# Loading the last y in two halves, and going over all PSUM banks once per half, in a batched matmul with transposed x

One Trainium2 chip, one core of it, one launch. The metric is the device time in microseconds of that core; the kernel before takes 261.97 us (median of 6 runs, 261.90 to 262.24).

## What is computed

```python
batch, m, k, n = 16, 512, 768, 1024
x: (batch, k, m) float32      y: (batch, k, n) float32
return np.einsum('bkm,bkn->bmn', x, y).astype(np.float32)
```

Inputs and output are float32 in HBM; the products are taken in bf16, which the comparison allows.

## The kernel before

PE is the matrix engine, DVE the vector engine, ACT the scalar engine; SP issues the transfers, which sixteen DMA engines carry out. PSUM is the memory, in banks, into which PE writes its sums. A transfer has *landed* when the last of the sixteen engines has reported its part. The *granted clock* is PE's clock as a share of full speed.

For each of 16 batches: x (1.57 MB) and y (3.15 MB) are loaded as one transfer each, cast to bf16 by DVE (one instruction for x, two for the halves of y), multiplied by PE into eight PSUM banks (six steps of the contraction for each), copied from PSUM by ACT, and stored (2.10 MB). All transfers are issued in program order by the SP queue. Stores are *held back*: that of batch b-4 is issued after the loads of batch b (`LAG`), so the loads never queue behind a store that is not ready yet.

```python
LAG = 4
...
for b in range(B):
    xs = xs_pool.tile([P, KT, M], FP32, name="xs")      # 2 buffers
    ys = ys_pool.tile([P, KT, N], FP32, name="ys")      # 2 buffers
    nc.sync.dma_start(xs[:], x_v[b])
    nc.sync.dma_start(ys[:], y_v[b])
    if b >= LAG:
        store(b - LAG)
    ...
    nc.vector.tensor_copy(x_sb[:], xs[:])
    for h in range(2):
        ks = slice(h * KT // 2, (h + 1) * KT // 2)
        nc.vector.tensor_copy(y_sb[:, ks], ys[:, ks])
    ...
    for mo in range(MT):                                # 4
        for nt in range(NT):                            # 2
            ns = slice(nt * NF, (nt + 1) * NF)
            ps = psum.tile([P, NF], FP32, name="ps")    # 8 banks
            for kt in range(KT):                        # 6
                nc.tensor.matmul(ps[:], x_w[:, kt, mo], y_sb[:, kt, ns],
                                 start=(kt == 0), stop=(kt == KT - 1))
            nc.scalar.copy(o_sb[:, mo, ns], ps[:])
for b in sorted(o_tiles):                               # the last LAG stores
    store(b)
```

## Time and profile before

| | kernel before |
|---|---|
| device time, median | 261.97 us |
| span of the profiled execution | 260.1 us |
| PE / DVE / ACT busy | 74% / 32% / 29% |
| share of the sixteen DMA engines | 98.5% |
| traffic | 109.05 MB |
| last y has landed | 235.0 us |
| last store issued, landed | 251.3 us, 259.2 us |

Three things to know when reading it. The span runs to the end of the program's last instruction, so the final wait for the stores is in it; the device time is about 1.9 us longer. The chain of waits ends earlier, with the last instruction that counts as busy, the last PSUM copy at 251.3. Waiting for a store and moving its data do not count: what the queue does after that copy has to be read from the windows and from the times that transfers take to land. And a transfer's issue is short (0.33 us) while its landing is late: the time in between contains everything that stood before it in the queue.

### The profile page before, as it was taken

What the parts mean: (1) busy time and instruction counts of PE and PEld (TensorE: products, weight loads), DVE (VectorE), ACT (ScalarE), POOL (GpSimd) and SP (SyncE); (2) the same over time, 40 slices, a digit from 0 to 9 for tenths busy, and PEclk for the clock granted to TensorE, in tenths of its full rate; (3) what the DMA queues carried; (4) which work ended last, traced back from release to release, by engine and by line L of the source; (5) the groups of instructions that cost most, each with busy time, mean ns of one, the idle gap of its engine ahead of it and who ended that gap; (6) DMA issues with size and microseconds to landing.
All of it is one profiled execution on the core that took longest, in us unless ns stands there. A gap on an engine that the chain in (4) does not pass through costs nothing.

```text
span 260.1 us, 1877 instructions
## 1 busy us (share of the span) xinstructions
PE 192.3 (74%) x768; PEld 89.3 (34%) x768; DVE 83.0 (32%) x48; ACT 76.4 (29%) x129; POOL 0.2 (0%) x4
## 2 busy tenths in 40 slices
PE   0059999896947939599597886939779395895950
PEld 0014555353523514235143342514334142351420
DVE  0271643525213252222524215252132522225000
ACT  1003444342421403314123241413324042141330
POOL 0000000000000000000000000000000000000000
PEclk9999999999997998959779797997999899796895
DMA  7999999999999999999999999999999999999995
GB/s 299 427 423 420 438 433 427 431 369 422 430 430 432 432 430 435 430 432 423 433 435 421 438 422 438 429 427 437 435 424 424 432 431 430 437 425 432 431 408 242
DMA packets 6921, 109.18 MB, mean 420 GB/s; under 512 B 768, under 2 KB 768, under 8 KB 768
## 3 DMA queue, kind: packets, MB, share of 16 engines
q1 hardware_dynamic: 6912, 109.05, 98.5%
q8 instruction: 6, 0.10, 0.1%
q14 instruction: 3, 0.02, 0.0%
HBM read 75.50 MB, written 33.55 MB: 419 GB/s over the span
## 4 chain that ended last, share of the span: by engine, by line
DMA 80%; DVE 10%; PE 5%; DVEq 1%; SPq 0%; issue 0%; ACT 0%
DMA ys<-in_y_dram 80%; DVE y_sb L65 10%; PE ps L74 5%; DVEq L106 1%; SPq L56 0%; ACT o_sb L76 0%; SPq L57 0%; DVEq L65 0%
## 5 line engine op out<-in xcount | busy, mean ns | idle before, releaser
L74 PE MATMUL ps<-y_sb,x_sb 128*128 128x512 bf16 x768 | 192.3, 413 | 58.4 <-DVE y_sb L65 58.4
L74 PEld LDWEIGHTS <-x_sb 128*128 128x128 bf16 x768 | 89.3, 118 | 160.9 <-issue 47.5
L76 ACT COPY o_sb<-ps 128x512 f32<-128x512 f32 x128 | 75.2, 587 | 174.1 <-PE ps L74 174.1
L65 DVE CAST y_sb<-ys 128x3072 bf16<-128x3072 f32 x32 | 54.9, 1757 | 89.4 <-DMA ys<-in_y_dram 89.4
L62 DVE CAST x_sb<-xs 128x3072 bf16<-128x3072 f32 x16 | 28.2, 1760 | 66.2 <-DMA xs<-in_x_dram 55.2
L76 ACT ACT_TABLE_LOAD x1 | 1.3, 1283 | 0.7 <-PEq L95 0.7
L95 POOL MEMSET const-uint8-127<- 128x1 uint8 x1 | 0.1, 103 | 0.0
L95 POOL MEMSET const-bfloat16-1.0<- 128x1 bf16 x1 | 0.1, 102 | 0.0
L95 POOL MEMSET const-float32-1.0<- 128x1 f32 x1 | 0.1, 100 | 0.0
L95 POOL MEMSET const-float32-0.0<- 128x1 f32 x1 | 0.1, 99 | 0.2 <-issue 0.2
## 6 DMA issues: line engine op xcount, KB each, us to landing
ys<-in_y_dram SPq DMA_DIRECT2D x16, 3072.0 KB, 28.1
out_dram<-o_sb SPq DMA_DIRECT2D x16, 2048.0 KB, 32.6
xs<-in_x_dram SPq DMA_DIRECT2D x16, 1536.0 KB, 29.7
```

The lines of the kernel that those rows point to most:

```text
L62: nc.vector.tensor_copy(x_sb[:], xs[:])
L65: nc.vector.tensor_copy(y_sb[:, ks], ys[:, ks])
L74: nc.tensor.matmul(ps[:], x_w[:, kt, mo], y_sb[:, kt, ns], start=(kt == 0), stop=(kt == KT - 1))
L76: nc.scalar.copy(o_sb[:, mo, ns], ps[:])
L95: nc = _bacc.Bacc("TRN2", target_bir_lowering=False, num_devices=1)
L106: with _tile.TileContext(nc) as tc:
```

## The change

The intent: at the end of the program nothing is left to load, so the last batch's cast, matmuls and copies stand alone (16.3 us after the last y). If its y comes in two halves, PE can do the first half of the contraction for all eight banks while the second half is still arriving.

```diff
+    KH = KT // 2
...
-            nc.sync.dma_start(xs[:], x_v[b])
-            nc.sync.dma_start(ys[:], y_v[b])
+            halves = 2 if b == B - 1 else 1
+            load(xs[:], x_v[b], 1)
+            for h in range(halves):
+                ks = slice(h * KT // halves, (h + 1) * KT // halves)
+                load(ys[:, ks], y_v[b, :, ks], 1)
...
-            for mo in range(MT):
-                for nt in range(NT):
-                    ns = slice(nt * NF, (nt + 1) * NF)
-                    ps = psum.tile([P, NF], FP32, name="ps")
-                    for kt in range(KT):
-                        nc.tensor.matmul(ps[:], x_w[:, kt, mo], y_sb[:, kt, ns],
-                                         start=(kt == 0), stop=(kt == KT - 1))
-                    nc.scalar.copy(o_sb[:, mo, ns], ps[:])
+            ps = {}
+            for h in range(halves):
+                for mo in range(MT):
+                    for nt in range(NT):
+                        if h == 0:
+                            ps[mo, nt] = psum.tile([P, NF], FP32, name="ps")
+                        for kt in range(h * KT // halves, (h + 1) * KT // halves):
+                            mm(ps[mo, nt], x_w, y_sb, kt, mo, nt)
+                        if h == halves - 1:
+                            nc.scalar.copy(o_sb[:, mo, nt * NF:(nt + 1) * NF], ps[mo, nt][:])
```

`load` and `mm` are the old calls under a name. Batches 0 to 14 are built as before.

More of the change, by code (lines that the diff above doesn't have):

```diff
@@ L45, with load, mm @@
     LAG = 4
+    KH = KT // 2
     o_tiles = {}
+    def load(dst, src, rows):
+        nc.sync.dma_start(dst, src)
     def store(b):
         nc.sync.dma_start(o_v[b], o_tiles.pop(b)[:])
+    def mm(ps, x_w, y_sb, kt, mo, nt):
+        nc.tensor.matmul(ps[:], x_w[:, kt, mo], y_sb[:, kt, nt * NF:(nt + 1) * NF],
+                         start=(kt == 0), stop=(kt == KT - 1))
     with tc.manual_schedule():
@@ L63 @@
             for h in range(2):
-                ks = slice(h * KT // 2, (h + 1) * KT // 2)
+                ks = slice(h * KH, (h + 1) * KH)
                 nc.vector.tensor_copy(y_sb[:, ks], ys[:, ks])
@@ L68 @@
             o_tiles[b] = o_sb
-            for mo in range(MT):
-                for nt in range(NT):
-                    ns = slice(nt * NF, (nt + 1) * NF)
-                    ps = psum.tile([P, NF], FP32, name="ps")
-                    for kt in range(KT):
-                        nc.tensor.matmul(ps[:], x_w[:, kt, mo], y_sb[:, kt, ns],
-                                         start=(kt == 0), stop=(kt == KT - 1))
-                    nc.scalar.copy(o_sb[:, mo, ns], ps[:])
-            if False:
-                store(b)
+            ps = {}
[8 more added lines that the diff above has]
+                            nc.scalar.copy(o_sb[:, mo, nt * NF:(nt + 1) * NF], ps[mo, nt][:])
         for b in sorted(o_tiles):
```

## The prediction

> **What bounds the kernel now.** I read the page from the top: engines, the DMA row, the chain of waits. Then I left the averages and went to the last 30 us, the only stretch that the change touches.
>
> ```profile
> span 260.1 us, 1877 instructions
> PE 192.3 (74%) x768; PEld 89.3 (34%) x768; DVE 83.0 (32%) x48; ACT 76.4 (29%) x129; POOL 0.2 (0%) x4
> DMA  7999999999999999999999999999999999999995
> q1 hardware_dynamic: 6912, 109.05, 98.5%
> HBM read 75.50 MB, written 33.55 MB: 419 GB/s over the span
> ```
>
> No compute engine is above 74%, while the sixteen DMA engines are busy in every slice between the first and the last, 98.5% of the span. 109.05 MB at the 430 GB/s of the middle slices is 253.6 us of a 260.1 us span. So the kernel is bound by its traffic, and the change moves the same bytes. A gain can come only from the 6.5 us that are not full-rate traffic: the start, and the end.
>
> The chain of waits, in order of time, cut to its end, seems to promise such a gain:
>
> ```profile
> 206.94 28.08 DMA ys<-in_y_dram
> 235.03 0.03 issue
> ...
> 235.12 1.76 DVE y_sb L65
> 236.88 1.68 DVEq L106
> 238.56 0.04 issue
> 238.60 12.09 PE ps L74 x45
> 250.69 0.02 issue
> 250.71 0.59 ACT o_sb L76
> ```
>
> The last y lands at 235.03, and 16.3 us of cast, matmuls and PSUM copies follow before the last store can be issued. But this chain ends with the last counted instruction, at 251.3; the span ends at 260.1, and the chain does not say what the queue carried between 235 and 260. Two further views do: the windows of the tail, and the stores that were issued in it.
>
> ```profile
> 219.30:235.03 15.73, 12.30 (x48) 5.63 (x48) 5.18 (x3) 4.70 (x8) 0.00 (x0) 0.89 1.01 432
> 235.03:251.00 15.97, 13.54 (x48) 5.76 (x48) 3.43 (x2) 4.40 (x8) 0.00 (x0) 0.79 1.00 426
> 251.00:252.50 1.50, 0.00 (x0) 0.00 (x0) 0.00 (x0) 0.29 (x1) 0.00 (x0) 1.00 0.85 360
> 252.50:257.00 4.50, 0.00 (x0) 0.00 (x0) 0.00 (x0) 0.00 (x0) 0.00 (x0) 0.59 0.97 411
> 257.00:258.60 1.60, 0.00 (x0) 0.00 (x0) 0.00 (x0) 0.00 (x0) 0.00 (x0) 0.50 0.29 123
> ```
>
> ```profile
> L50 SPq DMA_DIRECT2D out_dram<-o_sb x2: 333/333/333, 234.9 to 251.3; - x2
> ...
> DMA to landing us min/median/max: 7.9/13.7/19.5
> ```
>
> ```profile
> SPq L106 <- DMA out_dram<-o_sb: 7.3, 2, 4.8
> ```
>
> In the windows the last two figures are the DMA share and GB/s (before them stand the busy times, with their counts, and the granted clock). While PE works off the last batch, the queue runs at a share of 1.00: stores are held back by four batches, so those of batches 11 to 14 stand behind the last load and are written meanwhile. The second fence is two stores: that of batch 14, issued at 234.9, landing 19.5 us later at 254.4, and that of batch 15, issued at 251.3, landing 7.9 us later at 259.2. The third says the same from the other side: at the end the queue waits twice for stores, the longest 4.8 us, which is 259.2 less 254.4. A store is 2.097 MB, and at 432 GB/s that is 4.85 us. So the last store followed the one before it at the full rate: the queue, not the 16.3 us of compute, sets the end.
>
> **What the Trainium skill says.** "Perfetto Trace Analysis", section DMA Optimizations, makes splitting of transfers conditional: "If DMA engines are generally idle" smaller sections may let the task end sooner. Here they are not: 1.00 in the tail. "DMA: Bandwidth & Descriptors", section Queues, rings and completion order, says that each DMA engine takes its descriptors in ring order and that one copy is split over up to 16 rings. The trace agrees on the order: y of batch 13 landed at 203.39 by the chain, and behind it stood a store, x and y, then again a store, x and y; at 432 GB/s these take 2 x (4.85 + 3.64 + 7.28) = 31.5 us, which gives 234.9 for the last y, measured 235.03. "TensorE: Matmul & The Clock Gate", section What's actually happening, has two clocks, half after idleness and full after activity. The tail agrees in kind: after 2.70 us without matmuls, less than the page's window of some 3.4 us, the granted clock is 0.50 from 237 to 243, which stretches the last batch. "PSUM — Partial Sum Buffer", section The four PSUM rules, says the first matmul of a group clears the write bits of its whole bank. Eight groups open at once are therefore safe only with a bank each; 512 fp32 columns are one 2 KB bank and the pool has eight. No run shows it yet.
>
> **The change part by part.** Batches 0 to 14 keep instructions, transfers and order. I compared the built order of instructions: PE 768 matmuls and as many weight loads in both, ACT 128 copies, DVE 48 casts; only the DMA queue gets one more transfer, 49 in place of 48.
>
> 1. The last y as two transfers of 1.57 MB. These have the shape of an x load: 12 KB a partition and 8 partitions for each DMA engine. In the trace's packet records the median packet of 12 KB takes 460 ns, that of 24 KB 912 ns, so each engine takes 16 x 460 = 7.36 us in place of 8 x 912 = 7.30 us: +0.06 us, on the path. The issue, 0.33 us, lies under a backlog of 28 us.
>
> 2. The first half lands 16 x 460 / 2 = 3.7 us before the second: 231.4. DVE is idle there (its previous cast ended at 229.6), so its 1.76 us cast ends at 233.2. The second half lands at 235.1 and is cast by 236.9.
>
> 3. PE is in batch 14 until 234.2. Now the first 24 matmuls of batch 15 follow at once, not at 236.9. At full clock six matmuls take 1.29 us (copies of the steady part start 1.29 us apart), 0.216 each: 24 x 0.216 = 5.2 us, until 239.4. The second half has been cast for 2.5 us by then, so the other 24 run on to 244.6. Without the gap the clock should stay up; the old last batch took 13.8 us from 236.9, now 10.4 us from 234.2.
>
> 4. Copies: a bank is complete every 3 x 0.216 = 0.65 us and its copy takes 0.587 us, so ACT keeps up, the last ending at about 245.3. The last store is issued 6.0 us earlier than now.
>
> 5. None of these 6.0 us lies on what sets the end. The stores of batches 11 to 14 last until 254.4 whatever PE does, so the last store waits in the ring until its turn, and lands at 259.24 + 0.06 = 259.3. The sum: 261.97 + 0.06 = 262.03 us, in round figures 262.0.
>
> **The rivals.** *The compute tail shows in full.* Then 6.0 us go: 256 us, faster by 2.3%. For it: the chain of waits, whose last 16 us are compute. Against it: the share of 1.00 until 251 and the 4.8 us between the last two landings. With 8 MB of stores behind the last load I give it almost nothing.
>
> *The dip is recovered.* From 251.0 to 252.5 the rate falls to 360 GB/s: the last store came after the quickest engines had run dry. Missing are (431 - 360) x 1.5 us = 0.11 MB, 0.25 us of the whole queue. The change issues the store long before that and closes the dip. If the sixteen engines shared their work it would be worth 0.2 to 0.3 us, 261.7. Against it: each has a fixed share of the partitions, and the slowest decides. In the per-engine landings of the trace the first engine finishes store 14 at 251.4, the last at 254.4; that last one never ran dry, having landed store 13 at 249.56, store 14 at 254.41 and store 15 at 259.24, 4.85 and 4.83 us apart. Closing the dip makes fifteen engines wait longer for the sixteenth.
>
> *PE gets slower.* Every bank is visited twice, and the second visits may wait. If all 48 matmuls ran at half clock (0.43 us) from 234.2, PE would end at 254.8 and the last store be issued at 255.4; with its 7.9 us it would land at 263.3, 4 us late (266, 1.6% slower). Nothing speaks for that clock over 20 busy microseconds; there are 6 us of slack to the first engine's need and nearly 9 to the last one's.
>
> *Another share-out among the DMA engines.* The 3 us between first and last engine grew from 0.6 us at the start, in steps of about a microsecond on single engines. The page has 9 packets of the queues of kind "instruction"; if these cause the steps and fall otherwise in the new program, the slowest engine may end half a microsecond sooner or later.
>
> **Range and chances.** Predicted 262.0 us. Three runs of the kernel before lie within 0.2 us; adding 0.3 downwards for the dip and about 0.3 either way for the share-out gives 261.6 to 262.4. Two per cent would be 5.2 us, more than anything but the fallen first rival can give. Faster by over 2%: 0.01. Within 2%: 0.98. Slower: 0.01.
>
> **What would show it right or wrong.** Right: DVE casts the first half at about 231.4 and PE shows no gap near 235; last PSUM copy ends near 245.3 and the queue issues the last store there, but its time to landing grows from 7.9 to about 14 us; the last two landings stay 4.8 us apart; no dip near 251, with the fall of the rate at the very end starting over a microsecond earlier. Wrong: a span shorter by much more than 0.3 us with the last store landing well before 259, or any stretch of the tail where the queue was empty before the change, which I overlooked.

## The result

| | before | after |
|---|---|---|
| device time, median of 6 | 261.97 us (261.90 to 262.24) | 262.20 us (262.08 to 262.60) |
| ratio after / before | | 1.0008, 95% interval 0.9995 to 1.0021 |
| span of the profiled execution | 260.1 us | 260.5 us |
| last PSUM copy ends | 251.3 us | 245.65 us |
| last store issued | 251.3 us | 245.7 us |
| last store landed | 259.24 us | 259.63 us |

The same, then; the result is correct, with eight sums open at once in a bank each. Ratios are the mean time of one kernel's fast runs over that of the other's of the same rounds, so they are not quite the ratio of the medians quoted.

The chain of waits of the changed kernel, its last part (start, length, what):

```profile
219.63 3.44 DVE y_sb L78 x2
223.07 0.04 issue
223.11 21.93 PE ps L56 x93
245.04 0.02 issue
245.07 0.58 ACT o_sb L93
```

Before, this chain passed through the last load and its casts. Now the loads of the last batch are not in it: PE runs 93 matmuls without a wait from batch 14 into batch 15, and the last copy ends 5.65 us earlier. The timeline of the same stretch (start, length, engine, instruction; in brackets the idle time before it):

```profile
228.19 1.76 DVE L75 CAST x_sb<-xs 128x3072 bf16<-128x3072 f32 x1 [5.13 <-DMA xs<-in_x_dram]
...
231.85 1.76 DVE L78 CAST y_sb<-ys 128x3072 bf16<-128x3072 f32 x1 [1.91 <-DMA ys<-in_y_dram]
...
235.32 10.69 SPq L53 DMA_DIRECT2D out_dram<-o_sb  x2
235.44 1.76 DVE L78 CAST y_sb<-ys 128x3072 bf16<-128x3072 f32 x1 [1.83 <-DMA ys<-in_y_dram]
240.58 5.07 ACT L93 COPY o_sb<-ps 128x512 f32<-128x512 f32 x8 [5.29 <-PE ps L56]
```

Both casts lie under PE's work, and the eight copies follow one another. Everything that was wanted of PE, DVE and ACT happened. Now the queue: the windows that the prediction showed, of the changed kernel (the last two figures are DMA share and GB/s, before them the granted clock), then the two last stores, then the wait at the end:

```profile
235.03:251.00 15.97, 10.00 (x47) 4.99 (x45) 1.76 (x1) 4.96 (x9) 0.00 (x0) 0.89 1.02 433
251.00:252.50 1.50, 0.00 (x0) 0.00 (x0) 0.00 (x0) 0.00 (x0) 0.00 (x0) 0.50 0.92 393
...
257.00:258.60 1.60, 0.00 (x0) 0.00 (x0) 0.00 (x0) 0.00 (x0) 0.00 (x0) 0.50 0.31 133
```

```profile
L53 SPq DMA_DIRECT2D out_dram<-o_sb x2: 332/332/332, 235.3 to 245.7; - x2
...
DMA to landing us min/median/max: 13.9/16.7/19.5
```

```profile
SPq L121 <- DMA out_dram<-o_sb: 13.4, 1, 13.4
```

The last store is issued at 245.7 in place of 251.3 and takes 13.9 us to land in place of 7.9: 245.7 + 13.9 = 259.6. What PE gave, the queue took back as waiting; the queue's issuer now waits 13.4 us in one piece at the end. The engine that lands last had landed the store before at 254.81, 4.82 us earlier, the time of one store at full rate, as before (254.41, then 4.83). (These are the last of the sixteen landings of each store. That they belong to one engine is inferred, since a landing does not name its engine: the last but one keeps its distance, about 0.37 us over the last three stores before the change and about 0.44 us after.) The windows count a packet at its start, so they are uneven over a microsecond or two; the landings are the better evidence.

### The profile page after: what moved, and what is told of

It is laid out like the page before. It is cut to its first block, busy times and chain, and to the rows that moved or that the text cites. A ratio compares the mean times of both kernels' runs of the same rounds, so it can differ in the third digit from the quotient of the medians.

```text
span 260.5 us, 1879 instructions
## 1 busy us (share of the span) xinstructions
PE 191.3 (73%) x768; PEld 89.3 (34%) x768; DVE 83.1 (32%) x48; ACT 76.4 (29%) x129; POOL 0.2 (0%) x4
## 4 chain that ended last, share of the span: by engine, by line
DMA 74%; DVE 11%; PE 8%; issue 0%; ACT 0%; SPq 0%; DVEq 0%
DMA ys<-in_y_dram 74%; DVE y_sb L78 11%; PE ps L56 8%; ACT o_sb L93 0%; SPq L50 0%; DVEq L78 0%
```

## Experiments

If the compute tail is only hidden, and not without effect, it must show as soon as less is queued behind the last load. So the first four runs hold stores back by two batches in place of four. Two stores then stand behind the last y instead of four, and the loads end 9.8 us later (244.80 against 235.03 in the profiles). The rival is that the change gives nothing even there, because its halves do not overlap. The runs also take the change apart.

### 1. Kernel before, hold-back of two

```diff
-    LAG = 4
+    LAG = 2
```

> The kernel before, but stores held back by two batches in place of four, so two stores (batches 13 and 14) in place of four stand behind the last load. My theory (four queued stores hide the compute tail): loads end 2 x 4.85 us later, at 244.7; the old tail of 16.3 us puts the last store's issue at 261.0, and it lands 6.1 us later (the engines that had run dry took 6.1 us in the kernel before), at 267.1; with the 2.7 us between last landing and device time, 269.8 us (269 to 271). Rival (the tail costs nothing in any case): 262.

Measured: 269.33 us (268.47 to 270.83), 1.0289 of the kernel before (1.0247 to 1.0332). The windows of its tail, then its last two stores:

```profile
250.00:255.00 5.00, 5.00 (x25) 2.61 (x23) 0.00 (x0) 2.35 (x4) 0.00 (x0) 1.00 0.48 203
255.00:258.00 3.00, 3.00 (x16) 1.47 (x13) 0.00 (x0) 1.18 (x2) 0.00 (x0) 1.00 0.00 0
```

```profile
L50 SPq DMA_DIRECT2D out_dram<-o_sb x2: 332/338/343, 244.6 to 258.9; - x2
...
DMA to landing us min/median/max: 7.0/8.5/9.9
```

Here is the stretch that the kernel before does not have: from 255 to 258 the DMA moves nothing, 0 GB/s, while PE is busy throughout. The loads ended at 244.80 (expected 244.7), the last store was issued at 258.9 rather than 261.0, because PE's clock was at 1.00 in this execution's tail. Of the four runs two took 268.5 and two 270.2 and 270.8. That they are the ones with the halved clock is not shown: their mean clocks over the whole span, 0.899 and 0.901, are no lower than those of the two faster runs (0.891 and 0.903).

### 2. Changed kernel, hold-back of two

`LAG = 2` here too, in the changed kernel.

> The changed kernel with stores held back by two batches. My theory: the change does shorten the tail by about 5.7 us and here it shows: last store issued at about 255.4, landing 261.5, 264.2 us (263.5 to 265), that is 2% faster than the kernel before at the same hold-back. Rival (the change gives nothing even where the tail is exposed, because the halves do not overlap): 270, as the old one at two.

Measured: 264.44 us (263.29 to 265.34), 1.0094 (1.0056 to 1.0132).

```profile
250.00:255.00 5.00, 5.00 (x25) 2.63 (x24) 0.00 (x0) 3.49 (x6) 0.00 (x0) 1.00 0.48 205
255.00:258.00 3.00, 0.70 (x4) 0.12 (x2) 0.00 (x0) 1.20 (x3) 0.00 (x0) 1.00 0.41 175
```

```profile
L53 SPq DMA_DIRECT2D out_dram<-o_sb x2: 332/338/344, 246.0 to 256.4; - x2
...
DMA to landing us min/median/max: 6.3/7.4/8.6
```

The store resumes in the window where the old order stood still. The change is worth 4.9 us of the medians (269.33 - 264.44; expected 5.6), 1.8%, once the tail is exposed. Both kernels' runs fall into two groups, so compare like with like: fastest with fastest 5.2 us (268.47, 263.29), slowest with slowest 5.5 us (270.83, 265.34). The two profiles shown differ by only 3.2 us (268.47, 265.25), because the old order was caught with the clock up in its tail and the new one with a clock of 0.65 from 235 to 240. The rival falls.

### 3. and 4. Either half of the change alone, hold-back of two

Both edits are to the changed kernel, with `LAG = 2`.

Only the load in halves (PE bank by bank):

```diff
+            halves = 1
             for h in range(halves):
                 for mo in range(MT):
```

> Two batches held back; the last y in two transfers, but PE goes bank by bank as before. One half of the change alone. My theory: only the cast of the first half moves off the path (1.7 us), PE still waits for the second half's cast before its fourth matmul: 268.1 us, or down to 266 if PE's clock stays up over the shorter gap. If splitting the load were all that matters: 264.

Only PE's two passes (one load):

```diff
-            halves = 2 if b == B - 1 else 1
+            halves = 1
...
+            halves = 2 if b == B - 1 else 1
             ps = {}
```

> Two batches held back; the last y in one transfer, PE in two passes over the banks. The other half of the change alone. My theory: PE can only use the 1.7 us of the second half's cast, at half clock, where it did 3 matmuls and now does about 4: 269.5 us, 0.3 us or so below the old order. If the order of the passes were all that matters: 264.

Measured: load alone 267.91 us (266.18 to 268.25), 1.0216; passes alone 269.10 us (268.82 to 269.19), 1.0272. The chains of waits, PE's piece in the last batch, first of the old order (experiment 1), then of the load alone, then of the passes alone:

```profile
248.37 9.89 PE ps L74 x45
```

```profile
246.59 11.57 PE ps L56 x45
```

```profile
246.64 12.25 PE ps L56 x48
```

With the load alone PE does three matmuls of the first bank early, and 45 are left when the second half has been cast. They start 1.78 us earlier than in the old order, but this execution's clock was down for a part of them (0.76 from 245 to 250, against 1.00), so they end at 258.2 there and at 258.3 in the old order. With the passes alone it has nothing to do before the whole y is there, and all 48 are left. Against the old order at the same hold-back that is 1.4 and 0.2 us of the medians, together 1.6, while both at once give 4.9: the two parts need each other. Each of the two small figures is within the spread of the old order's own runs (268.47 to 270.83).

### 5. and 6. How much slack there is: 24 more matmuls in the last batch, hold-back of four

The kernel before computes its last four banks twice; the changed kernel does its first pass twice. Results are unchanged and correct.

```diff
-                    for kt in range(KT):
-                        nc.tensor.matmul(...)
+                    for rep in range(2 if b == B - 1 and mo >= MT // 2 else 1):
+                        for kt in range(KT):
+                            nc.tensor.matmul(...)
```
```diff
+                        if halves == 2 and h == 0:
+                            for kt in range(KH):
+                                nc.tensor.matmul(..., start=(kt == 0), stop=(kt == KH - 1))
                         for kt in range(h * KT // halves, (h + 1) * KT // halves):
```

> The kernel before with 24 extra matmuls in the last batch (the last four PSUM banks are computed twice; the result is unchanged), 24 x 0.216 = 5.2 us more on PE after the last load. My theory: in the kernel before, the issue of the last store (251.3) is less than 2 us ahead of the moment when it would set the end (254.4 plus 4.8, less the 6.3 to 7.0 us that a store needs when it meets an empty queue, so about 252.5). With 5.2 us more it is issued at 256.5, lands at 262.8 to 263.5, and the time is 265.5 to 266.3 us, if the granted clock takes the same course; 263.5 if the clock stays up. Rival (the tail has no influence at all at a hold-back of four): 262.

> The changed kernel with 24 extra matmuls in the last batch (the first pass over the eight banks is done twice; result unchanged). My theory: the change has bought 5.6 us of slack and this uses it up: last store issued at 250.9, before the queue needs it; time unchanged, 262.2 us (262.0 to 262.6). Rival (the earlier issue is of no use as slack): 265.

Measured: before with the dose 263.71 us (263.21 to 264.34), 1.0070 (1.0045 to 1.0095); changed with the dose 261.97 us (261.65 to 262.18), 1.0005 (0.9990 to 1.0020). The two windows in which they differ, first the kernel before with the dose, then the changed one:

```profile
251.00:252.50 1.50, 1.50 (x9) 0.78 (x8) 0.00 (x0) 0.54 (x1) 0.00 (x0) 1.00 0.62 262
252.50:257.00 4.50, 2.02 (x10) 0.82 (x8) 0.00 (x0) 0.64 (x2) 0.00 (x0) 1.00 0.32 138
```

```profile
251.00:252.50 1.50, 0.00 (x0) 0.00 (x0) 0.00 (x0) 0.00 (x0) 0.00 (x0) 1.00 1.05 448
252.50:257.00 4.50, 0.00 (x0) 0.00 (x0) 0.00 (x0) 0.00 (x0) 0.00 (x0) 0.57 0.90 386
```

In the first the queue runs dry while PE still works; its last store is issued at 255.2 and lands 6.3 us later, at 261.4, 2.2 us after that of the kernel before. The added 5.2 us of work cost so little because 1.6 us were slack (259.24 less 6.3 is 252.9, the latest harmless issue; the issue was at 251.3), and because PE's clock was partly up where it had been halved: 0.72 from 236.9 to 243.0, against 0.50. In the changed kernel the same dose is free: its last store is issued at 250.4.

### 7. and 8. Hold-back of three

Both kernels with `LAG = 3`.

> The kernel before with stores held back by three batches: loads end at 239.9, the last store is issued at about 256.2 (253.8 if the clock stays up in the tail) and lands 6.3 to 7.0 us later, 262.8; 265.5 us, between 263 and 266. The tail is exposed by some 3 us.

> The changed kernel with stores held back by three batches: last store issued at 250.6, while the store before it is still being written until 254.4 on the slowest engine; hidden again, 262.2 us (262.0 to 262.6). With the change a hold-back of three is as good as one of four.

Measured: before 264.81 us (262.95 to 264.88), 1.0097 (1.0062 to 1.0132); changed 262.32 us (262.08 to 262.45), 1.0018 (1.0003 to 1.0033). The old order issues its last store at 255.9, into an empty queue, and it lands at 262.2; the changed one issues it at 250.0, while the store before is still being written (until 254.9), and it lands at 259.7. With the change, three held-back stores hide the tail to within 0.2%. That should let one of the five output buffers go (16 KB of each partition; not tried), and saves no time.

### 9. and 10. Either half alone, hold-back of four

The edits of 3 and 4, with `LAG = 4`.

> Hold-back of four as in both kernels; the last y in two transfers, PE bank by bank as before. This is the only part of the change that touches the queue. If the extra transfer costs its packets (16 x 460 ns for 8 x 912 ns), the last y lands 0.06 us later and the time is 262.0 to 262.2, not to be told from the kernel before. If splitting as such disturbs the queue: 263 or more.

> Hold-back of four; the last y in one transfer, PE in two passes. Nothing on the queue changes; the last store is issued up to a microsecond before or after 251.3, both hidden: 261.9 to 262.2 us. The passes themselves would be a cost if this ran over 262.5.

Measured: load alone 261.78 us (261.59 to 262.25), 1.0000 (0.9985 to 1.0015); passes alone 261.93 us (261.77 to 262.10), 1.0003 (0.9988 to 1.0018). Neither costs anything that can be measured.

### 11. Half of the matmuls left out

Wrong result (relative error 0.71): every second step of the contraction only.

```diff
-                    for kt in range(KT):
+                    for kt in range(0, KT, 2):
...
-                                         start=(kt == 0), stop=(kt == KT - 1))
+                                         start=(kt == 0), stop=(kt == KT - 2))
```

> Wrong result on purpose: the kernel before with only every second step of the contraction, 384 matmuls in place of 768, all transfers kept. My theory (the queue sets the time, PE is out of it): half of PE's work is worth nothing, 261.9 to 262.1 us. The one thing that could make it faster is the spread of the sixteen DMA engines: if its steps come from the fetching of PE's instructions (6 packets of that kind on the page, here 3), the last landing comes 0.5 to 1 us earlier: 261.0 to 261.5. Rival (PE's 74% matter somewhere in the steady part): 255 or less.

Measured: 261.88 us (261.44 to 262.14), 0.9996 (0.9983 to 1.0010). From the head of its page, the span and the row of the engines:

```profile
span 259.9 us, 1109 instructions
...
PE 119.8 (46%) x384; PEld 46.8 (18%) x384; DVE 83.0 (32%) x48; ACT 76.4 (29%) x129; POOL 0.2 (0%) x4
```

PE at 46% in place of 74%, and the same time: nowhere in this kernel does PE set the pace. The side theory, that fewer instruction fetches would bring the end 0.5 to 1 us forward, fails for the time, though one step of the spread does move. DVE's cast of x of batch 3, which needs all sixteen engines, first in the kernel before, then here:

```profile
41.17 1.76 DVE L62 CAST x_sb<-xs 128x3072 bf16<-128x3072 f32 x1 [1.48 <-DMA xs<-in_x_dram]
```

```profile
40.01 1.76 DVE L62 CAST x_sb<-xs 128x3072 bf16<-128x3072 f32 x1 [0.29 <-DMA xs<-in_x_dram]
```

In the packet records of the kernel before, an instruction packet of 16 KB occupies an engine for 1.02 us at 37.6 us, and one engine lands 1.2 us late from then on (spread between first and last engine 1.83 us, before that 0.62). With half of the matmuls the first such packet comes at 54.8, and at 41 us the spread is 0.60. But by the last store but one it has grown to 2.68 us all the same, against 3.05, and the last landing is at 259.06, against 259.24. The landings show when the spread grows in the kernel before: 0.62 to 1.83 us with the packet at 37.6, then 1.83 to 2.96 us between 50.2 and 58.1, where no instruction packet lies, and hardly after that, although five more packets of 16 KB follow (after each of them a landing other than the last one moves back). What the second step is stays open.

No version here beats the kernel before by more than noise, and none of the experiments points to one: 109 MB at 430 GB/s leave 6.5 us of a 260.1 us span. The first packet of data moves at 1.7 us, and the span ends 0.8 us after the last landing; that the spread of the engines takes most of the rest is my reading and was not shown.

## Why the prediction was right

It said 262.0 us, 261.6 to 262.4; 262.20 was measured. By its steps:

1. *Last y in two transfers, +0.06 us.* In the landings of the trace, x and y of the last batch are 7.29 us apart before (227.74, 235.03) and 3.70 + 3.66 = 7.36 us after (228.06, 231.76, 235.42): +0.07 us.
2. *Casts at 231.4 and 235.1.* Measured 231.85 and 235.44. Of the 0.4 us, 0.33 was there when x of the last batch was cast (228.19 against 227.86), before anything had changed.
3. *PE to 244.6.* Measured 245.04, so 0.1 us off beyond the shift; the granted clock stayed at 1.00 over the point where PE had stood still.
4. *Last copy at 245.3, store 6.0 us earlier.* Measured 245.65 and 5.6 us earlier; again the shift.
5. *None of it on what sets the end.* Store landed at 259.63, predicted 259.3; the last two landings of the slowest engine 4.82 us apart. Experiments 1 to 8 show the reason rather than the coincidence: with two or three stores behind the last load the tail is exposed and the change gains, with four it is hidden.

The rivals: *the tail shows in full* would have been nearly right at a hold-back of two, where 4.9 of the 6.0 us appear. *The dip is recovered*: the first engine did finish the last store 1.2 us earlier (256.22 against 257.43) and the last did not, so the dip closed and brought nothing. *Another share-out* may be what is left of the difference, but that is not shown: the slowest engine was 0.32 us later than in the kernel before already at the last x, and 0.22 us later already at the very first (7.10, 6.88). The profiles of three runs with the whole change (the changed kernel, experiments 6 and 8) end with a spread of 3.41 to 3.45 us at the last store but one, the others at a hold-back of three or four with 2.68 to 3.14; why stays open. The interval of the ratio does not say that the kernels differ at all. *PE gets slower* did not happen, and its sum had one wrong term: I let a store take 7.9 us from issue to landing wherever it met an empty queue. That was the figure of a store whose slowest engine still had the one before to finish; alone it takes 6.3 to 7.0 us (experiments 1 to 5 and 7). With these the landing of that rival comes at 261.7 to 262.4 in place of 263.3.

## What to carry to other kernels

Before shortening a tail of compute, look at what the queue is carrying in that stretch, and at how far apart the last two transfers land: if that is the bare time of one transfer, the tail is already hidden and its shortening turns into waiting. A chain of waits that ends in compute is no proof, since data movement after the last busy instruction is not in it. Early loads and an order of work that can use them are one change, not two: each alone gave at most 1.4 us where both gave 4.9.

## What the Trainium skill lacked or had wrong

- "TensorE: Matmul & The Clock Gate", section What's actually happening, gives an idle window of about 3.4 us before the clock halves and calls the window "free-running". Here a gap of 2.70 us was followed by a granted clock of 0.50 from 237 to 243 (kernel before), and one of 2.77 us by 1.00 throughout (kernel before, hold-back of two). In the first case the clock records put the fall at 236.26, only 2.03 us after the last matmul had ended. So a gap shorter than the window can halve the clock or not; the page's table, with at least one idle window as the condition, reads as if it could not.
- "DMA: Bandwidth & Descriptors", section Anatomy of one DMA — SWDGE (gpsimd) path, fits about 2.0 us plus bytes at 436 GB/s to a transfer on that path. I found no such figure for stores from SP: 2.10 MB into an empty queue took 6.3 to 7.0 us here, so 1.5 to 2.2 us beyond the 4.81 us that are an estimate by that page's rate.
- No page gives a figure for how far the sixteen engines drift apart in a long stream from SP: the first and the last of them landed 0.62 us apart at the start and 3.05 us at the last store but one of the kernel before, so closing a dip of the mean rate brought nothing. One step of 1.2 us coincides with a 16 KB instruction packet at 37.6 us, and was absent at 41 us in experiment 11, where the first such packet comes at 54.8 us; another, of 1.1 us, has no such packet beside it.
- "Perfetto Trace Analysis", section DMA Optimizations, makes splitting conditional on generally idle engines. This leaves out what decided here. The engines were busy while the halves loaded at a hold-back of four, where the split alone gave a ratio of 1.0000, and just as busy at a hold-back of two (share 1.02 from 240 to 245), where splitting gave 1.8% together with the order that uses it. The difference was whether the queue would run dry later, before the last store was ready.
